# Lag rows of an S5 mixer fetched within on-chip memory, contraction rows by channel then row, later factor sums as plain DMA sums

## The chip, the cores and the metric

The kernel runs on one core of one Trainium2 chip. The metric is the device time of one execution in microseconds (us). A core has TensorE (PE; its weight loads are listed apart as PEld), VectorE (DVE), ScalarE (ACT), GpSimd (POOL) and SyncE (SP), which work through separate instruction queues and wait for each other by semaphores. DMAs are issued from the queues of SP, ACT and POOL.

## The reference, cut to what matters

One layer of a backbone: an S5 mixer (a diagonal complex state-space model, run in both directions over 256 context and 1024 latent positions, 64 groups of 16 channels with 64 states each) with GELU and a gate, then a SwiGLU feed-forward part. The mixer's core:

```python
lam_bar = jnp.exp(lam * jnp.exp(log_step)[:, None])
b_bar = ((lam_bar - 1.0) / lam)[..., None] * lax.complex(b_re, b_im)
def run(u, h0):
    bu = jnp.einsum('lgh,gnh->lgn', u, b_bar)
    bu = bu.at[0].add(lam_bar * h0)
    a = jnp.broadcast_to(lam_bar, bu.shape)
    _, h = lax.associative_scan(_linear_combine, (a, bu), axis=0)
    return jnp.einsum('lgn,ghn->lgh', h, c_mat).real, h[-1]
...
y = y_forward + y_backward + d_skip * h
g = gelu(y)
g = g * sigmoid(g @ w_glu + b_glu)
...
return (silu(h @ w1) * (h @ w3)) @ w2
```

All data are float32, and around both parts stand RMS norms and shifts, scales and gates made from c and c_ctx through ada_w.

## The kernel before, in words

The 1024 latent positions are 128 chunks of T = 8 rows. A chunk's 8 rows by 16 channels of one group are 128 numbers, which is the contraction axis of the matmuls around the scan. So the recurrence goes over chunks, with powers of lam_bar to the 8th as steps, and what happens inside a chunk is done by matrices.

Four stages follow each other. **To 30 us** parameters and inputs are loaded. **30 to 121** prepares: powers of lam_bar, the input matrices (BL, made by bl_make at line 407 as products of a factor BXY, repeated over the 8 rows, and a power table LB or its bank copies LBP, repeated over the 16 channels), their transposes, and the chunk inputs of the scan. Of the products of 128x1024, those of the hb values in PMUL run on POOL, the others on DVE. **121 to 221** is the scan: scan() (line 899) lays all its steps into DVE's queue, one dependent product and sum after another. Under it the other engines prepare what turns states into outputs. **221 to 252** takes the late half of the states, GELU and the transposes; **252 to 999** is the gate and the feed-forward part.

The order of the work under the scan is written out by hand in the string PROG1, of which each word is a step that issues its instructions on every engine concerned, and each engine takes its own in that order. PROG2 does the same behind the scan. The steps that matter here:

- C (cl_ops, line 679), on POOL: makes the output factors CL of quarter q, direction d. A group of five: a product, a product, an addition, a product, an addition. How the two additions are done is written in HOWS, two letters for each direction of each quarter: E is an operation on POOL, Y an accumulating DMA issued by POOL, P two pairs of matmuls with an identity on PE (line 693) that ACT copies back (line 694). q prepares the sum or difference of the factors of a quarter and, for q2, the power sums pw_sums(1) (line 620).
- K (k_mats, line 835), K0 to K7: two per quarter. PE computes from CL and BBn the impulse response of 16 channels for 15 lags, 240 numbers per row; ACT copies two such blocks from PSUM into the buffers KX (line 854) and stores them in a DRAM tensor kd (line 855).
- T (toeplitz, line 858), T0 to T15: SP loads from kd, over DRAM, the eight shifted windows of 128 numbers that make a 128 x 128 matrix of lags for four groups (line 863, 256 KB), into one of four KQ buffers in RA.
- P, P0 to P5: PE multiplies early states by CL (line 975, states_mm) and the chunk's own rows by KQ (line 999, x_mm); R copies states for it (line 955, ACT); Y copies the result out (line 1057, ACT). F fills in states on POOL. A computes adaLN rows on PE from ada_w pieces that SP loads (line 523). L loads the factors of C on ACT's queue (line 667).
- Behind the scan: Z copies the late half of the states (line 957 on DVE, 955 on ACT), N multiplies them by CL (line 975), D adds, H applies GELU (line 1066), I and J are transposes and Q covers groups 6 and 7.

SP's and ACT's DMAs share eight semaphores, which the program gives out in turn, in the order of the program text over both queues; a DMA waits until the one that had its semaphore before has landed.

Of the kernel before, what the change touches and what calls it, by code (L numbers as in the profile page):

```python
# [17 lines left out]
P = 128  # L18
# [24 lines left out]
def s5_ffn_kernel(tc, a, out):  # L43
# [3 lines left out]
    with ctx:  # L47
# [56 lines left out]
        modb = small([6, T])[:, 0:2]  # L104
        nrm = small([2, T])
        S5 = int(round(pos[0] * 256))
# [218 lines left out]
        S.activation(rsb, rsb, AF.Sqrt, bias=epsc[:, 0:1], scale=1.0 / D)  # L325
        LB = view(RC[2], 8, [2, T, P])

        def lb_dup(d, i, pt):

            pt = pt.rearrange("p (s g) -> p s g", s=T)  # L330
            PE.matmul(pt, cid[:, d], CP[:, :, i] if d else CP[:, ::-1, i], start=True, stop=True)
            S.activation(LB[:, i, :, G * d:G * d + G], pt, AF.Copy, scale=sgn[:, 0:1] if i else 1.0)

# [62 lines left out]

        BL1 = [view(RC[1], 4 * i, [8, T, HC]) for i in range(3)] + [view(RC[0], 8 + 4 * i, [8, T, HC]) for i in range(2)]
        BL2 = [view(r, kb, [8, T, HC]) for r, kb in ((RC[1], 12), (RXc, 4), (RC[3], 4))]
        Win = [view(RC[r], kb, [2, 4, P]) for r, kb in ((3, 0), (2, 0), (2, 4))]
        BB = view(RC[3], 8, [2, G, HC])  # L400

        def bls(hb):
            return BL1[hb % 5], BL2[hb % 3]

        def bl_make(hb, o2=None):

            if hb >= 16:
                return
            b, d = bd(hb)
            es = slice(64 * d + 8 * b, 64 * d + 8 * b + 8)  # L410
            for i in range(2):
                l_ = bc((LBP[hb][:, i] if hb in LBP else LB[:, i, :, es]).rearrange("p s g -> p g s"), 3, HC)
                tt(o2 if i and o2 is not None else bls(hb)[i], bc(BXY[:, b // 2 % 2, i, d, 8 * (b % 2):8 * (b % 2) + 8], 2, T), l_, MUL, E if hb in PMUL else V)

        LBP = {}

        def lb_psum(hb, eng=V):

            n, o = {0: (0, 0), 2: (0, 128), 4: (1, 384), 7: (0, 0), 9: (0, 128), 11: (1, 384), 12: (2, 384), 14: (0, 0),
                    15: (0, 128)}[hb]  # L420
            bank = (lbt, LTa, tq)[n]
            b, d = bd(hb)
            LBP[hb] = bank[:, o:o + 128].rearrange("p (i s g) -> p i s g", i=2, s=T)
            src = LB[:, :, :, 64 * d + 8 * b:64 * d + 8 * b + 8]
            if eng is S:
                S.copy(LBP[hb], src)
            else:
                eng.tensor_copy(LBP[hb], src)
# [8 lines left out]
        def bl_tr(hb, copy=True):  # L437
            b, d = bd(hb)
            t1 = bls(hb)[0]
            pt, w_ = pv2(), Win[hb % 3]  # L440
            for j in range(2):
                for i in range(4):
                    PE.transpose(pt[:, j, P * i:P * i + P], t1[:, 4 * j + i].rearrange("p s h -> p (s h)"), ident)
            if not copy:
                return pt, w_
            if hb == 15:
                S.copy(w_[:, 0].rearrange("p i n -> p (i n)"), pt[:, 0])
                V.tensor_copy(w_[:, 1].rearrange("p i n -> p (i n)"), pt[:, 1])
            else:
                S.copy(w_.rearrange("p j i n -> p (j i n)"), pt.rearrange("p j n -> p (j n)"))  # L450
            bb_copy(hb)

        def bb_copy(hb):
            b, d = bd(hb)
            S.copy(BB[:, d, 8 * b:8 * b + 8], bls(hb)[0][:, :, 7 if d == 0 else 0])

# [86 lines left out]
        pr0 = pv2()  # L543
        o2 = pr0.rearrange("p j (i s h) -> p (j i) s h", i=4, s=T)
        bl_make(0, o2)
# [127 lines left out]
        def cs_sum(q):  # L673
            c0, c1, c2 = (Cs[q % 2][:, i].rearrange("p d g h -> p (d g h)") for i in range(3))
            tt(c2, c0, c1, SUB, E)

        MB = view(RXa, 0, [D])

        def cl_ops(q, d):
# [8 lines left out]
            def add(o, how, last):  # L688
                if how == "P":
                    for h in range(2):  # L690
                        hs, pc = slice(4 * h, 4 * h + 4), pw([512])
                        for i, src in enumerate((o, ct)):
                            PE.matmul(pc, ident, src[:, hs].rearrange("p g t h -> p (g t h)"), start=i == 0, stop=i == 1)
                        S.activation(o[:, hs].rearrange("p g t h -> p (g t h)"), pc, AF.Copy, scale=-1.0 if last else 1.0)
                elif how == "Y":
                    E.dma_start(o, ct, accum_op=ADD)
                else:
                    tt(o, o, ct, SUB if last else ADD, E)

# [135 lines left out]
        def k_mats(q, hq, kts):  # L835
# [16 lines left out]
            for g_ in range(2):  # L852
                gq, kx = 2 * hq + g_, KX[2 * hq + g_]
                S.copy(kx, kts[g_])
                S.dma_start(KD_[q][:, gq], kx)

        def toeplitz(u):

            q, gi = divmod(u, 4)
            rows = KD_[q][32 * gi:32 * gi + HC]  # L860
            n = 15 * HC
            src = bass.AP(rows.tensor, rows.offset, [[HC, T], [n, 4 * HC], [1, P]])
            SY.dma_start(KQ[u % 4], src)

# [143 lines left out]
        def run(prog):  # L1008


            for w in prog.split():
# [784 lines left out]
def layouts(i):  # L1796
# [3 lines left out]
    ident = np.eye(P, dtype=np.float32)  # L1800
    blk = np.kron(np.eye(8, dtype=np.float32), np.ones((HC, HC), np.float32))
# [4 lines left out]
    sel = np.tile(np.eye(HC, dtype=np.float32), (8, 8))  # L1806
    msk = np.kron(np.eye(8, dtype=np.float32), np.ones((HC, 1), np.float32))
# [42 lines left out]
```

## Time and profile before

| | us |
|---|---|
| median of 3 runs | 1009.99 |
| lowest and highest | 1006.97, 1013.54 |
| the profiled execution | 1006.91 |
| its span, first to last instruction | 1005.1 |
| mean granted TensorE clock | 0.984 |
| busy: PE, PEld | 952.8, 751.5 |
| busy: DVE, POOL, ACT | 774.3, 748.7, 427.7 |

The profile is of one execution. A row of a group gives line, engine, operation, tiles written and read (buffer numbers left out), the shapes, the count, the busy time, the mean duration in ns and the idle time of the engine just before such instructions, with what ended it. L77 is the helper tt, through which almost all elementwise operations go, so groups of L77 are told apart by their tiles. A timeline row begins with its start and its length, and an idle time in brackets stands before it. ACTq, SPq and POOLq are issues of DMAs.

### The profile page before, as it was taken

Reading aid. Unit: us, or ns where it says so; the run is one execution under the profiler, and the core shown is the slowest. Engines: PE = TensorE matmul, PEld = TensorE weight load, DVE = VectorE, ACT = ScalarE, POOL = GpSimd, SP = SyncE. Lnnn points to the kernel's source line nnn. Section 1 sums busy time; section 2 is a strip of 40 time slices with the busy share of each in tenths; the row PEclk is TensorE's granted clock in tenths of the full one; section 3 lists DMA queues with packets and bytes.
Section 4 is the critical chain, followed back from the end, with each engine's and each line's share of the span. In section 5 each row is a group of like instructions: output and inputs, shape, how many; then the busy total and the mean of one; then the engine's idle time right before and its main releaser. Section 6 shows DMA issues by size and latency. Waiting matters only on the chain. (4 is left out here: it accounts for less than half of the span.)

```text
span 1005.1 us, 17726 instructions
## 1 busy us (share of the span) xinstructions
PE 952.8 (95%) x6604; PEld 751.5 (75%) x6604; DVE 774.3 (77%) x1630; ACT 427.7 (43%) x808; POOL 748.7 (74%) x595
## 2 busy tenths in 40 slices
PE   5987898879999999999999999999999999999996
PEld 1466535769888778778888888888888888888885
DVE  7979899984556778878869586685958677686977
ACT  5478622224434563343233343434243343334337
POOL 5799998963734458979786869777785878777764
PEclk9999998889999999999999999999999999999999
DMA  9765998535520032011212121111212120111205
GB/s 335 285 133 108 287 316 273 125 85 171 210 64 22 1 105 84 11 43 42 74 53 74 42 79 34 47 61 45 74 42 84 43 64 32 61 55 53 74 22 167
DMA packets 49118, 99.95 MB, mean 99 GB/s; under 512 B 4348, under 2 KB 18940, under 8 KB 47752
## 3 DMA queue, kind: packets, MB, share of 16 engines
q1 hardware_dynamic: 43416, 86.64, 26.1%
q0 software_dynamic: 2592, 9.44, 5.1%
q10 hardware_dynamic: 3024, 2.74, 0.9%
q8 instruction: 52, 0.85, 0.3%
q14 instruction: 34, 0.28, 0.1%
HBM read 83.20 MB, written 6.17 MB: 89 GB/s over the span
## 5 line engine op out<-in xcount | busy, mean ns | idle before, releaser
L77 POOL TENSOR_TENSOR c<-rxc,c 128x512 fp32r<-128x512 f32 x127 | 166.0, 1320 | 52.3 <-ACT c L1305 51.5
L1364 PE MATMUL ut<-ra,c 128*128 128x512 f32 x400 | 155.7, 389 | 1.2 <-DVE ra L77 1.2
L1363 PE MATMUL ut<-ra,c 128*128 128x512 f32 x400 | 155.7, 389 | 0.2 <-ACT ra L1305 0.2
L1365 PE MATMUL ut<-ra,c 128*128 128x512 f32 x400 | 155.6, 389 | 0.0
L1305 ACT CAST c<-rxc 128x512 fp32r<-128x512 f32 x128 | 79.0, 622 | 147.6 <-PE xt L1658 53.0
L1658 PE MATMUL xt<-c,c 128*128 128x512 f32 x540 | 129.7, 389 | 0.0
L77 DVE TENSOR_TENSOR ru<-ru,xt 128x1024 f32<-128x1024 f32 x90 | 107.9, 1216 | 13.4 <-PE xt L1658 9.4
L1658 PEld LDWEIGHTS xt<-c,c 128*128 128x128 f32 x540 | 101.4, 188 | 21.0
L77 DVE TENSOR_TENSOR ru<-ut,ru 128x512 f32<-128x512 f32 x98 | 67.2, 686 | 44.1 <-PE ut L1365 38.6
L1364 PEld LDWEIGHTS ut<-ra,c 128*128 128x128 f32 x400 | 75.1, 188 | 17.1 <-POOL rxc L77 1.5
L1363 PEld LDWEIGHTS ut<-ra,c 128*128 128x128 f32 x400 | 75.1, 188 | 16.1 <-ACT ra L1305 0.6
L1365 PEld LDWEIGHTS ut<-ra,c 128*128 128x128 f32 x400 | 75.1, 188 | 15.6
L77 POOL TENSOR_TENSOR c<-ru,c 128x512 fp32r<-128x512 f32 (+1 forms) x39 | 58.8, 1507 | 10.1 <-ACT c L1305 5.7
L77 POOL TENSOR_TENSOR rxc<-rxc 128x512 f32<-128x512 f32 (+1 forms) x44 | 63.8, 1450 | 2.2 <-ACT rxc L671 0.6
L77 POOL TENSOR_TENSOR c<-rw,c 128x512 fp32r<-128x512 f32 (+1 forms) x28 | 37.4, 1337 | 37.5 <-ACT c L1305 37.5
L1363 PE MATMUL ut<-c,c 128*128 128x512 f32 x160 | 62.3, 390 | 0.8 <-DVE rxa L77 0.8
L1364 PE MATMUL ut<-c,c 128*128 128x512 f32 x160 | 62.3, 389 | 0.0
L1365 PE MATMUL ut<-c,c 128*128 128x512 f32 x160 | 62.2, 389 | 0.0
L1658 PE MATMUL ut<-c,c 128*128 128x512 f32 x216 | 51.9, 389 | 0.0
L77 DVE TENSOR_TENSOR ru<-ru,ut 128x512 f32<-128x512 f32 x76 | 47.3, 680 | 0.7 <-ACT ru L1712 0.5
L1658 PEld LDWEIGHTS ut<-c,c 128*128 128x128 f32 x216 | 40.5, 188 | 8.4
L587 PE MATMUL pv<-ru,c 128*64 128x160 f32 x512 | 41.4, 312 | 5.2 <-ACT c L450 2.0
(453 smaller groups left out, 2392.0 us busy)
## 6 DMA issues: line engine op xcount, KB each, us to landing
c<-in_ada_w SPq DMA_DIRECT2D x46, 256.0 KB, 5.9
rxc<-in_w SPq DMA_DIRECT2D x38, 256.0 KB, 2.9
rxc<-in_w SPq DMA_DIRECT2D x19, 512.0 KB
c<-c POOLq DMA_DIRECT2D x11, 512.0 KB, 5.7
ru<-in_w SPq DMA_DIRECT2D x11, 512.0 KB
rw<-in_w SPq DMA_DIRECT2D x11, 512.0 KB, 3.6
ra<-in_ada_w SPq DMA_DIRECT2D x10, 512.0 KB, 10.8
ra<-in_ada_w SPq DMA_DIRECT2D x18, 256.0 KB, 8.8
```

Of the source, the lines that this page charges most:

```text
L77: eng.tensor_tensor(out=o, in0=x, in1=y, op=op)
L587: PE.matmul(pv[64 * (i % 2):64 * (i % 2) + 64, ri, c0:c0 + 160], w[:, i, 64 * ri:64 * ri + 64], U[:, 8 * b + 4 * j + i], start=True, stop= ...
L1305: S.copy(o[0], x)
L1363: PE.matmul(pu, wh, bh, start=start, stop=False)
L1364: PE.matmul(pu, wh, bl, start=False, stop=False)
L1365: PE.matmul(pu, wl, bh, start=False, stop=stop)
L1658: PE.matmul(pd, w[:, cs_], b, start=j in (1, 2, 4) and n == 0, stop=n == 2, skip_group_check=j not in (1, 2, 4))
```

## The change

The lag rows no longer pass through DRAM. KX becomes two buffers that hold both blocks of one K step (in R0 and RW), and 64 DMAs of 64 KB fetch the shifted windows from there straight into KQ; T and t words (groups hq 0 and 1) issue them on SP, and the new words e (behind K0) and f (behind K1) issue the first sixteen on ACT. The tensor kd is gone. For this the 128 contraction rows are ordered by channel, then row, where they were by row, then channel: in LB, BL1, BL2, LBP, bl_make's broadcasts, the views around transposes, and the tables xT, ctxT, blk and sel, which are laid out before the kernel starts. HOWS uses DMA additions in quarters 2 and 3 where it had operations on POOL or matmuls; there the factors are prepared with signs that make every addition plain. The power sums of quarters 2 and 3 (word n1) are issued earlier and take two operations on POOL and a negation on ACT where they took four on POOL. Words of PROG1 stand in another order.

```diff
-HOWS = "YPYP EPEP YEYE YPYE"
+HOWS = "YPYP EPEP YYYY YYYE"
...
-PROG1 = ("A22 G1 B0 A26 A30 C01 O0 C03 q1 A34 K0 O1 A38 A42 C10 C11 K1 O2 L2 A46 A50 C12 C13 A54 K2 O3 A58 T0 T1 T2 T3 F10 F11 G2 R0 K3 L3 R1 P0 Y0 Y1 A64 M0 P1 T4 T5 R2 Y2 Y3 G3 q2 C20 T6 T7 C21 P2 R3 Y4 Y5 C22 M1 P3 Y6 Y7 C23 q3 C30 K4 K5 R4 T8 T9 T10 T11 C31 C32 C33 F30 F31 P4 R5 Y8 Y9 K6 P5 Y10 Y11 K7 T12 T13 T14 T15 w0 l1 M2 m0 w1")
+PROG1 = ("A22 G1 B0 A26 A30 C01 O0 C03 q1 A34 K0 e0 e1 e2 e3 O1 A38 A42 C10 C11 K1 O2 L2 f0 f1 f2 f3 A46 A50 C12 C13 n1 A54 K2 O3 A58 F10 F11 G2 R0 K3 L3 R1 P0 Y0 Y1 T4 T5 t4 t5 A64 M0 P1 R2 Y2 Y3 T6 T7 t6 t7 G3 q2 C20 C22 C21 P2 R3 Y4 Y5 M1 P3 Y6 Y7 C23 q3 C30 K4 T8 T9 T10 T11 K5 t8 t9 t10 t11 R4 C31 C32 C33 F30 F31 P4 R5 Y8 Y9 K6 T12 T13 P5 Y10 Y11 T14 T15 K7 t12 t13 t14 t15 w0 l1 M2 m0 w1")
...
-        LB = view(RC[2], 8, [2, T, P])
+        LB = view(RC[2], 8, [2, P, T])
...
-        BL1 = [view(RC[1], 4 * i, [8, T, HC]) for i in range(3)] + [view(RC[0], 8 + 4 * i, [8, T, HC]) for i in range(2)]
+        BL1 = [view(RC[1], 4 * i, [8, HC, T]) for i in range(3)] + [view(RC[0], 8 + 4 * i, [8, HC, T]) for i in range(2)]
...
-                l_ = bc((LBP[hb][:, i] if hb in LBP else LB[:, i, :, es]).rearrange("p s g -> p g s"), 3, HC)
-                tt(o2 if i and o2 is not None else bls(hb)[i], bc(BXY[:, b // 2 % 2, i, d, 8 * (b % 2):8 * (b % 2) + 8], 2, T), l_, MUL, E if hb in PMUL else V)
+                l_ = bc(LBP[hb][:, i] if hb in LBP else LB[:, i, es], 2, HC)
+                tt(o2 if i and o2 is not None else bls(hb)[i], bc(BXY[:, b // 2 % 2, i, d, 8 * (b % 2):8 * (b % 2) + 8], 3, T), l_, MUL, E if hb in PMUL else V)
...
-            tt(PS[i], PWF[:, :, 0, :, gs], PWF[:, :, 1, :, gs], ADD, E)
-            if i == 0:
-                tt(PWF[:, :, 1, :, gs], PWF[:, :, 1, :, gs], PWF[:, :, 0, :, gs], SUB, E)
-            else:
-                for d, gs, neg in ((slice(0, 2), slice(16, 24), True), (slice(0, 1), slice(24, 32), False), (slice(1, 2), slice(24, 32), True)):
-                    re, im = PWF[:, :, 0, d, gs], PWF[:, :, 1, d, gs]
-                    tt(im, re if neg else im, im if neg else re, SUB, E)
+            re, im = PWF[:, :, 0, :, gs], PWF[:, :, 1, :, gs]
+            tt(PS[i], im, re, SUB if i else ADD, E)
+            tt(im, im, re, ADD if i else SUB, E)
+            if i:
+                S.activation(im, im, AF.Copy, scale=-1.0)
...
-            tt(c2, c0, c1, SUB, E)
+            tt(c2, c0, c1, ADD if q > 1 else SUB, E)
...
-        KX = [cpk[:, HC + P:HC + P + 15 * HC], cols.rearrange("p a b g -> p (a b g)")[:, 0:15 * HC]]
-        KX += [view(RW, 4 + i, [15 * HC]) for i in range(2)]
+        KX = [R0[:, 32 + P:32 + P + 30 * HC], view(RW, 4, [30 * HC])]
+        KX = [t.rearrange("p (g x) -> p g x", g=2) for t in KX]
         KQ = [view(RA, STB * (2 + i // 2) + 2 * (i % 2), [4, P]) for i in range(4)]
-        KD_ = [dr.tile([P, 4, 15 * HC], F32, tag=f"kd{q}", name=f"kd{q}") for q in range(4)]
...
-                gq, kx = 2 * hq + g_, KX[2 * hq + g_]
-                S.copy(kx, kts[g_])
-                S.dma_start(KD_[q][:, gq], kx)
-
-        def toeplitz(u):
-
-            q, gi = divmod(u, 4)
-            rows = KD_[q][32 * gi:32 * gi + HC]
-            n = 15 * HC
-            src = bass.AP(rows.tensor, rows.offset, [[HC, T], [n, 4 * HC], [1, P]])
-            SY.dma_start(KQ[u % 4], src)
+                S.copy(KX[hq][:, g_], kts[g_])
+
+        def toeplitz(u, hq, eng=SY):
+
+            for g_ in range(2):
+                rows = KX[hq][32 * (u % 4):32 * (u % 4) + HC, g_]
+                src = bass.AP(rows.tensor, rows.offset, [list(rows.ap[0]), [HC, T], [1, P]])
+                eng.dma_start(KQ[u % 4][:, 2 * hq + g_], src)
...
-                    toeplitz(i)
+                    toeplitz(i, int(op in "tf"), S if op in "ef" else SY)
```

Three places of the queues show how the rows move. In the rows below c_63 to c_66 are the four 16 KB regions that hold the factors, r_60 is a parameter region, kt and pw are PSUM tiles; line numbers of the changed kernel are smaller by 2 to 8 from line 620 on.

On ACT, behind the matmuls of K0. Before:

```order
L854 COPY r_60<-kt 128x240
L855 DMA kd_1250<-r_60 128x240
L854 COPY r_60<-pw 128x240
L855 DMA kd_1250<-r_60 128x240
L804 COPY pw<-r_60 128x240
L694 ACTIVATE c_64<-pw 128x512 x2
```

Now:

```order
L850 COPY r_60<-kt 128x240
L850 COPY r_60<-pw 128x240
L857 DMA ra<-r_60 128x1x128 x8
L802 COPY pw<-r_60 128x240
L692 ACTIVATE c_64<-pw 128x512 x2
```

Two stores give way to eight fetches, which stand ahead of the zeroing of the next PSUM tile (802) and the copies of the next P addition (692).

On POOL, the two directions of quarter 2. Before:

```order
L77 TENSOR_TENSOR c_66<-rxc,rxa 128x1024
L77 TENSOR_TENSOR c_65<-rxc 128x1024
L696 DMA c_65<-c_66 128x1024
L77 TENSOR_TENSOR c_65<-rxc,rxa 128x1024
L77 TENSOR_TENSOR c_65<-c_65,c_66 128x1024
L77 TENSOR_TENSOR c_66<-rxc,rxa 128x1024
L77 TENSOR_TENSOR c_65<-rxc 128x1024
L696 DMA c_65<-c_66 128x1024
L77 TENSOR_TENSOR c_65<-rxc,rxa 128x1024
L77 TENSOR_TENSOR c_65<-c_65,c_66 128x1024
```

Now:

```order
L77 TENSOR_TENSOR c_66<-rxc,rxa 128x1024
L77 TENSOR_TENSOR c_65<-rxc 128x1024
L694 DMA c_65<-c_66 128x1024
L77 TENSOR_TENSOR c_66<-rxc,rxa 128x1024
L77 TENSOR_TENSOR c_65<-rxc 128x1024
L694 DMA c_65<-c_66 128x1024
L77 TENSOR_TENSOR c_65<-rxc,rxa 128x1024
L694 DMA c_65<-c_66 128x1024
L77 TENSOR_TENSOR c_65<-rxc,rxa 128x1024
L694 DMA c_65<-c_66 128x1024
```

The two additions on POOL are DMAs, and the first halves of both directions come ahead of the second halves. In quarter 3 one more DMA takes the place of the matmuls below.

On PE, between K5 (its last two matmuls are the first two rows; pm and kt are its PSUM tiles) and K6. Before:

```order
L850 MATMUL kt<-rxc,rxa 16x16
L850 MATMUL pm<-rxc,rxa 16x16
L693 MATMUL pw<-c_66,r_60 128x512
L693 MATMUL pw<-ra,r_60 128x512
L693 MATMUL pw<-c_66,r_60 128x512
L693 MATMUL pw<-ra,r_60 128x512
L975 MATMUL pw<-c_65,ra 64x128 x32
L999 MATMUL pw<-ra,ru 128x128 x8
```

Now:

```order
L847 MATMUL kt<-rxc,rxa 16x16
L847 MATMUL pm<-rxc,rxa 16x16
L967 MATMUL pw<-c_65,ra 64x128 x32
L991 MATMUL pw<-ra,ru 128x128 x8
L839 MATMUL kt<-c_66,rxa 16x112
L839 MATMUL pm<-c_66,rxa 16x112
```

P4 (967, 991) follows K5 at once, and K6 (839) follows P4 as before. DVE's rows are the same in the same order in both kernels.

More of the change, by code (lines that the diff above doesn't have):

```diff
@@ L96, in small @@
             return v
+        nrm = small([2, T])
         cpk = small([HC + 3 * P + HC + 4 + T + 16 + 8])
@@ L104, in s5_ffn_kernel @@
         modb = small([6, T])[:, 0:2]
-        nrm = small([2, T])
         S5 = int(round(pos[0] * 256))
@@ L331, in lb_dup @@
             PE.matmul(pt, cid[:, d], CP[:, :, i] if d else CP[:, ::-1, i], start=True, stop=True)
-            S.activation(LB[:, i, :, G * d:G * d + G], pt, AF.Copy, scale=sgn[:, 0:1] if i else 1.0)
+            S.activation(LB[:, i, G * d:G * d + G].rearrange("p g s -> p s g"), pt, AF.Copy, scale=sgn[:, 0:1] if i else 1.0)
         for i in range(2):
@@ L395, in bd @@
             return divmod((0, 2, 1, 3)[hb] if hb < 4 else hb, 2)
-        BL1 = [view(RC[1], 4 * i, [8, T, HC]) for i in range(3)] + [view(RC[0], 8 + 4 * i, [8, T, HC]) for i in range(2)]
-        BL2 = [view(r, kb, [8, T, HC]) for r, kb in ((RC[1], 12), (RXc, 4), (RC[3], 4))]
+        BL1 = [view(RC[1], 4 * i, [8, HC, T]) for i in range(3)] + [view(RC[0], 8 + 4 * i, [8, HC, T]) for i in range(2)]
+        BL2 = [view(r, kb, [8, HC, T]) for r, kb in ((RC[1], 12), (RXc, 4), (RC[3], 4))]
         Win = [view(RC[r], kb, [2, 4, P]) for r, kb in ((3, 0), (2, 0), (2, 4))]
@@ L422, in lb_psum @@
             b, d = bd(hb)
-            LBP[hb] = bank[:, o:o + 128].rearrange("p (i s g) -> p i s g", i=2, s=T)
-            src = LB[:, :, :, 64 * d + 8 * b:64 * d + 8 * b + 8]
+            LBP[hb] = bank[:, o:o + 128].rearrange("p (i g s) -> p i g s", i=2, s=T)
+            src = LB[:, :, 64 * d + 8 * b:64 * d + 8 * b + 8]
             if eng is S:
@@ L442, in bl_tr @@
                 for i in range(4):
-                    PE.transpose(pt[:, j, P * i:P * i + P], t1[:, 4 * j + i].rearrange("p s h -> p (s h)"), ident)
+                    PE.transpose(pt[:, j, P * i:P * i + P], t1[:, 4 * j + i].rearrange("p h s -> p (h s)"), ident)
             if not copy:
@@ L454, in bb_copy @@
             b, d = bd(hb)
-            S.copy(BB[:, d, 8 * b:8 * b + 8], bls(hb)[0][:, :, 7 if d == 0 else 0])
+            S.copy(BB[:, d, 8 * b:8 * b + 8], bls(hb)[0][:, :, :, 7 if d == 0 else 0])
         r4, mx = view(RA, 74, [4, P]), view(RA, 76, [2, 2, 32])
@@ L543, in s5_ffn_kernel @@
         pr0 = pv2()
-        o2 = pr0.rearrange("p j (i s h) -> p (j i) s h", i=4, s=T)
+        o2 = pr0.rearrange("p j (i h s) -> p (j i) h s", i=4, s=T)
         bl_make(0, o2)
@@ L693, in add @@
                             PE.matmul(pc, ident, src[:, hs].rearrange("p g t h -> p (g t h)"), start=i == 0, stop=i == 1)
-                        S.activation(o[:, hs].rearrange("p g t h -> p (g t h)"), pc, AF.Copy, scale=-1.0 if last else 1.0)
+                        S.activation(o[:, hs].rearrange("p g t h -> p (g t h)"), pc, AF.Copy, scale=-1.0 if last and q < 2 else 1.0)
                 elif how == "Y":
@@ L697, in add @@
                 else:
-                    tt(o, o, ct, SUB if last else ADD, E)
+                    tt(o, o, ct, ADD, E)
             h0, h1 = HOWS.split()[q][2 * d:2 * d + 2]
@@ L1026, in run @@
                     cs_sum(i)
-                    if i == 2:
-                        pw_sums(1)
+                elif op == "n":
+                    pw_sums(i)
                 elif op == "B":
@@ L1040, in run @@
                     fill(*divmod(i, 10), *((RXc, 0) if i >= 30 else (RC[3], 12)))
-                elif op == "T":
-                    toeplitz(i)
+                elif op in "Ttef":
+                    toeplitz(i, int(op in "tf"), S if op in "ef" else SY)
                 elif op == "R":
@@ L1800, in layouts @@
     ident = np.eye(P, dtype=np.float32)
-    blk = np.kron(np.eye(8, dtype=np.float32), np.ones((HC, HC), np.float32))
+    blk = np.kron(np.ones((HC, HC), np.float32), np.eye(8, dtype=np.float32))
     pat = np.tile(np.eye(HC, dtype=np.float32), (8, 1))
@@ L1805, in layouts @@
     sg[:64, 1], sg[64:, 1] = 1, -1
-    sel = np.tile(np.eye(HC, dtype=np.float32), (8, 8))
+    sel = np.tile(np.repeat(np.eye(HC, dtype=np.float32), 8, 1), (8, 1))
     msk = np.kron(np.eye(8, dtype=np.float32), np.ones((HC, 1), np.float32))
@@ L1823, in layouts @@
     a["x"] = c(f["x"][0])
-    a["xT"] = c(f["x"].reshape(P, T, G, HC).transpose(1, 3, 2, 0).reshape(P, G, P))
-    a["ctxT"] = c(f["ctx"].reshape(32, T, G, HC).transpose(1, 3, 2, 0).reshape(P, G, 32))
+    a["xT"] = c(f["x"].reshape(P, T, G, HC).transpose(3, 1, 2, 0).reshape(P, G, P))
+    a["ctxT"] = c(f["ctx"].reshape(32, T, G, HC).transpose(3, 1, 2, 0).reshape(P, G, 32))
     a["ada_w"] = c(f["ada_w"][0])
```

## The prediction, on record before the run

> **What bounds the kernel now.** I read the windows of the four stages first, then the groups of VectorE in the stage that the edits touch, then the chain of waits of TensorE and the timeline of three engines around that stage's end. In the windows the columns are: from and to, length, then the busy time of PE, PEld, DVE, ACT and POOL, the granted TensorE clock, the share of the DMA engines and GB/s.
>
> ```profile
> 30.00:121.00 91.00, 75.72 (x744) 53.57 (x744) 81.54 (x192) 63.88 (x142) 85.19 (x95) 0.98 0.71 183
> 121.00:221.00 100.00, 88.51 (x1708) 53.20 (x1701) 99.45 (x559) 25.75 (x56) 92.28 (x80) 0.88 0.73 217
> 221.00:252.00 31.00, 29.27 (x833) 28.12 (x810) 13.10 (x23) 14.54 (x21) 9.19 (x9) 1.00 0.50 147
> 252.00:999.00 747.00, 740.67 (x3310) 611.23 (x3308) 554.03 (x742) 307.18 (x570) 547.94 (x398) 1.00 0.19 61
> ```
>
> TensorE is busy for 740.67 of the last 747 us, and no instruction of that stretch is edited. Nearly all that the change edits lies under 121 to 221, where VectorE, the scan, is busy for 99.45 of 100 us. Its two largest shapes show that it waits for nobody (the last column is the idle time ahead of them):
>
> ```profile
> L77 DVE TENSOR_TENSOR ltc<-ra,lta 128x128 f32<-128x128 f32 x92 | 26.7, 290 | 0.0
> L77 DVE TENSOR_TENSOR ltb<-ra,lta 128x128 f32<-128x128 f32 x92 | 26.6, 289 | 0.1
> ```
>
> So 100 us of this stage are VectorE's alone, and what TensorE, ScalarE, GpSimd or a DMA saves under it can show only at its end. There:
>
> ```profile
> 220.82 0.29 DVE L77 TENSOR_TENSOR ra<-ltc,ra 128x128 f32<-128x128 f32 x1
> 221.25 0.76 DVE L957 COPY ra<-ra 128x512 f32<-128x512 f32 x2
> ```
> ```profile
> 222.39 0.36 ACT L854 COPY rw<-kt 128x240 f32<-128x240 f32 x1 [0.78 <-PE pm L850]
> ...
> 223.59 0.47 ACTq L855 DMA_DIRECT2D kd<-rw  x1
> 224.11 1.14 ACT L955 COPY ra<-ra 128x512 f32<-128x512 f32 x2 [0.54 <-ACT rw L854]
> ```
> ```profile
> 222.81 1.32 PE L975 MATMUL pe<-c,ra 64*64 64x128 f32 x33 [0.47 <-ACT rw L854]
> 224.97 7.26 PE L975 MATMUL pe<-c,ra 64*64 64x128 f32 x227 [0.85 <-issue]
> ```
>
> The scan ends at 221.1. The last work under it, K7, is copied out at 222.39, and the first late product N0 begins at 222.81 after a wait for that copying. N0 needs Z0, the first of the two copies on DVE: 221.25 plus half of 0.76 is 221.63. TensorE is thus about 1.1 us behind the scan at the handover, and this little, not the 100 us, is open to the change.
>
> **The change part by part.** *Lag rows.* Sixteen stores into kd and sixteen loads from it go. TensorE waited for them as follows:
>
> ```profile
> PE pw L999 <- DMA ra<-kd: 5.5, 4, 3.6
> ```
> ```profile
> 209.43 2.08 PE L999 MATMUL pw<-ra,ru 128*128 128x128 f32 x8 [3.55 <-DMA ra<-kd]
> 212.12 2.08 PE L999 MATMUL pw<-ra,ru 128*128 128x128 f32 x8 [0.61 <-DMA ra<-kd]
> ```
>
> 5.5 us in all, 3.55 and 0.61 of it in P4, the only place after which the end of K7 can move. In their place come 64 copies of 64 KB within SBUF. No such copy stands in the trace; the nearest rows are these (durations of an issue as least, median, most):
>
> ```profile
> L863 SPq DMA_DIRECT2D ra<-kd x16: 574/640/3513, 166.5 to 228.3; - x16
> L855 ACTq DMA_DIRECT2D kd<-rw x8: 326/326/940, 153.2 to 223.6; - x8
> ```
> ```profile
> DMA to landing us min/median/max: 2.7/3.3/5.0
> ```
> ```profile
> c<-in_ada_w SPq DMA_DIRECT2D x46, 256.0 KB, 5.9
> ra<-in_ada_w SPq DMA_DIRECT2D x18, 256.0 KB, 8.8
> ```
>
> An issue costs between 0.33 and 0.64 us, a landing between 2.7 us (the least of the 120 KB stores) and 8.8 us. I take 0.4 and 4, near the store, since that also leaves SBUF in short rows and is the closer in size. One hop in place of store and load then ends P4's two waits.
>
> The Trainium skill, "DMA: Bandwidth & Descriptors", section "Rules for kernel authors", speaks against this edit: many small transfers should be put together, and under 64 KB one pays mostly overhead. Its section "Bandwidth" gives 0.95 us for 64 KB; eight in a row would by that estimate land 7.6 us after the first began, which would give P4 its wait back but still leave K7 about where it was, and the sum no gain. No trace here shows such a copy.
>
> *The sums.* TensorE loses the four matmuls of the one addition that stands between K5 and P4, at half clock:
>
> ```profile
> 197.74 2.08 PE L693 MATMUL pw<-c,r 128*128 128x512 f32 x2 [0.57 <-POOL c L77]
> ...
> 203.62 0.41 PE L975 MATMUL pw<-c,ra 64*64 64x128 f32 x4
> ```
>
> That is 5.9 us. GpSimd, busy 92.28 of 100, loses two additions and gains three DMA issues:
>
> ```profile
> L77 POOL TENSOR_TENSOR c<-c,rw 128x1024 f32<-128x1024 f32 x2 | 4.7, 2356 | 0.2
> L696 POOL DMA_DIRECT2D c<-c x3 | 2.6, 875 | 0.9 <-POOL c L77 0.6 <-DMA ra<-kd 0.3
> L77 POOL TENSOR_TENSOR rxa<-rxa 128x64 f32<-128x64 f32 x2 | 0.6, 320 | 0.0
> L77 POOL TENSOR_TENSOR rxa<-rxa 128x128 f32<-128x128 f32 x1 | 0.5, 454 | 0.1
> ```
>
> 2 x 2.36 less 3 x 0.88 is 2.1 us saved, and the power sums, four operations now two and a negation on ScalarE, save some 0.4 more. Nobody on the path waits for that; the cover is the scan. The new wait is that K4 to K7 now read sums that a DMA finishes, and that landing takes:
>
> ```profile
> c<-c POOLq DMA_DIRECT2D x4, 512.0 KB, 7.8
> ...
> c<-ra POOLq DMA_DIRECT2D x1, 512.0 KB, 4.7
> ```
>
> K4 stands behind P2 and P3 in TensorE's order; before K6 the very last step stays an addition on GpSimd. I let 0 to 3 us of it reach TensorE.
>
> *ScalarE's queue.* Eight fetches each now sit in it after K0 and K1, ahead of the evacuations that TensorE needs for C11, K1 and C13. The program hands all hardware DMAs eight semaphores in turn over both queues, so each of the 16 waits until the DMA eight before it has landed, and those ahead are the 256 KB loads above. Sixteen issues of 0.33 to 0.64 are 5.3 to 10.2 us against 16 issues of kd stores saved later (5.2); waits for landings come on top. I put TensorE 0 to 8 us late at K2 to P3, 4 taken.
>
> *K7's end* is then 222.3 - 5.9 - 3.55 - 0.6 = 212.2, plus 0 to 8 for ScalarE's queue and 0 to 3 for the landings: 212 to 223, taken 216 to 217. In most of this span TensorE ends before the scan, and the waits that were removed come back as one idle stretch in front of N0.
>
> *The order of rows.* Same sizes on every engine; the two broadcast operands of the products of 128x1024 change places, so that now the first one repeats along the innermost axis. There are 18 of them on DVE in the second stage (10 of the next row's kind, and eight with other tiles):
>
> ```profile
> L77 DVE TENSOR_TENSOR c<-c,lbt 128x1024 f32<-128x1024 f32 x10 | 11.9, 1218 | 4.1 <-DMA c<-c 3.3 <-DVE lbt L428 0.4
> L77 DVE TENSOR_TENSOR ra<-ltb,r 128x64 f32<-128x64 f32 x4 | 0.7, 219 | 0.1
> L77 DVE TENSOR_TENSOR ra<-ra,ltb 128x64 f32<-128x64 f32 x4 | 0.9, 214 | 0.0
> ```
>
> The second row (the scales spread at line 473) already repeats its first operand along the innermost axis and takes 219 ns against 214 of a plain one of its size. Ends: nothing, or at worst 18 x 1.22 = 22 us if each took double. I take nothing, by the near row.
>
> *After the scan.* Gains: N0 at 221.7 and not 222.81, 1.1 us. ScalarE's second pair of state copies, held to 224.11 behind K7's copies and stores, can follow the scan at once, so that the idle 0.85 inside N0 should go too: 1.95 together, as the upper end 2.4 with a further issue gap of 0.41 at 240.3.
>
> ```profile
> PE pe L988 <- issue: 0.4, 1, 0.4
> ```
>
> Against it stands the clock:
>
> ```profile
> 168.20:171.60 3.40, 3.40 (x64) 3.12 (x64) 3.40 (x21) 1.30 (x3) 3.40 (x3) 0.50 0.69 198
> 205.70:209.10 3.40, 0.18 (x6) 0.00 (x0) 3.26 (x16) 0.00 (x0) 3.40 (x4) 1.00 0.63 134
> 209.10:212.50 3.40, 2.46 (x10) 2.16 (x11) 3.40 (x21) 0.00 (x0) 3.24 (x6) 0.51 0.58 148
> 212.50:215.90 3.40, 3.40 (x97) 3.14 (x98) 3.40 (x21) 1.08 (x2) 3.32 (x6) 0.50 0.20 58
> 215.90:219.30 3.40, 3.40 (x132) 3.25 (x132) 3.40 (x21) 0.72 (x2) 3.22 (x7) 0.99 0.14 40
> 222.80:226.20 3.40, 2.54 (x72) 2.46 (x76) 0.00 (x0) 2.44 (x4) 0.00 (x0) 1.00 0.23 75
> ```
> ```profile
> 216.47 2.27 PE L975 MATMUL pw<-c,ra 64*64 64x128 f32 x64
> ```
>
> A stretch of 3.4 us with almost no matmul (205.7) is followed by two at half clock, while one with 2.54 of 3.4 is not. 64 matmuls of one kind take 3.40 us at 0.50 and 2.27 at 0.99, so a third of the time at half clock is lost. If TensorE idles from 216.5 to 221.7, the start of N0 runs at half clock for one to two stretches, 3.4 to 6.8 us, and 1.1 to 2.3 us are lost, 1.7 in the middle. The Trainium skill, "TensorE: Matmul & The Clock Gate", Part 1, has the windows free-running; which of the two ends comes is then left to their phase, which this trace doesn't settle for another kernel.
>
> **Sum.** -1.1 - 0.85 + 1.7 = -0.25 us, with ends at -2.4 (no half clock, all gaps gone) and +1.2 (2.3 lost, only 1.1 gained). The profiled execution took 1006.91 us (span 1005.1 and 1.8 around it): 1006.7. It is 3.1 below the median of the runs, 1009.99, and I see no part of that difference that the change would take away; so 1009.7 for a median.
>
> **Rivals.**
> A. *No half clock*: K7 ends only after 218 or so, or the idle stretch does not fill a window. Then -2.0 to -2.4, 1007.7. For it: landings of 7.8 us above, which would hold K6. Against: 10 us have been taken from TensorE's chain.
> B. *ScalarE's queue sets the end* (slower): the sixteen waiting fetches push K1 to K7 later than the scan by themselves. This decides once the delays exceed the 10 us removed less the 1.2 us lag, about 9; with landings of 8.8 us met twice, 17.6 us late, K7 would end at 229.8 and N0 start seven us late, less the 0.85: +6, 1016. For it: ScalarE has evacuations of TensorE behind these waits. Against: the scan's slack absorbs the first nine.
> C. *The broadcast in the other operand is slow*: 22 us on DVE before the scan, +22, 1032. Against: the row of 219 ns.
> D. *The kernel before loses time in some runs to the trip over DRAM* (its runs spread over 6.6 us), and the change removes that: 1007. Nothing in one profile can show it.
>
> **How the numbers follow.** A measurement of this kernel tells about 1% from no change, 10.1 us. The main case has 0.60, A 0.12, D 0.14, B 0.09, C 0.04, and 0.01 is left for a gain before the scan that I don't see. Main, A and D lie within 1%; of B a quarter goes beyond, C wholly. So faster 0.01, same 0.93, slower 0.06. The range goes from 1004.5 (the lowest run, 1006.97, less 2.4) to 1015 (the highest run, 1013.54, plus 1.2, and just short of B).
>
> **What would show it.** Right: no TensorE wait for a DMA in P4; K7's last copy near 217 and an idle stretch of 4 to 9 us that ends at Z0; half clock after it; the scan ending at 221 as before; the last stage unchanged. Wrong: K7's copies after 221 again (A, or B with a ScalarE that waits for DMAs between 147 and 170), the 128x1024 products above 1.22 us (C), or a scan that ends more than 1 us earlier or later, since nothing of the sum allows that.

## The result, and the profile after

The changed kernel is slower: 1014.62 us median of 19 runs (1009.08 to 1022.08) against 1007.03 for the kernel before (1004.14 to 1013.54, 19 runs), a ratio of the means of 1.0065 with a 95% interval of 1.0047 to 1.0084, or 4.7 to 8.5 us. The time lies inside the range given, by 0.4 us, but the forecast of no change doesn't hold: the loss is small and clear. The profiled execution took 1015.43, with a span of 1013.7 against 1005.1.

The windows of the changed kernel, with the columns as above, for the scan and for the stretch behind it:

```profile
121.00:221.00 100.00, 78.91 (x1426) 44.64 (x1418) 99.39 (x557) 21.71 (x50) 84.76 (x69) 0.85 0.80 208
221.00:252.00 31.00, 28.66 (x863) 26.96 (x866) 12.77 (x21) 15.02 (x22) 8.12 (x14) 1.00 0.54 134
```

VectorE is as busy under the scan as before. TensorE got 78.91 us of work done there and not 88.51. A part of that is the matmuls of the addition that is gone; but from 221.00 to N0 at 232.75 TensorE is still busy for 9.71 us with the rest of P4, with K6, P5 and K7, which stood under the scan before but for the end of K7. The ends of the three engines' work there:

```profile
220.10 0.29 DVE L77 TENSOR_TENSOR ra<-ltc,ra 128x128 f32<-128x128 f32 x1
220.52 1.75 DVE L949 COPY ra<-ra 128x512 f32<-128x512 f32 x2
```
```profile
222.36 1.29 ACT L1049 COPY ru<-pw 128x512 f32<-128x512 f32 x2 [6.60 <-PE pw L991]
...
232.34 0.36 ACT L850 COPY rw<-kt 128x240 f32<-128x240 f32 x1 [0.97 <-ACT ru L1049]
232.59 0.36 ACT L850 COPY rw<-pm 128x240 f32<-128x240 f32 x1
```
```profile
232.75 1.56 PE L967 MATMUL pe<-c,ra 64*64 64x128 f32 x41 [0.52 <-ACT rw L850]
```

The scan ends at 220.4, a little earlier than before. K7's last copy starts at 232.6 where it started at 223.2, and N0, which waits for the first of K7's two copies, starts at 232.75 (222.81 before). So the whole loss is this: TensorE's work under the scan no longer fits under it. The chain of waits names two kinds of waiting that are new or larger; the columns are engine and line, releaser, us in total, times, longest:

```profile
PE pw L991 <- DMA ra<-rw: 9.5, 6, 3.3
...
ACT c L692 <- DMA ra<-rw: 9.8, 1, 9.8
...
ACT pw L802 <- DMA ra<-r: 7.6, 1, 7.6
```

TensorE waits 9.5 us for lag rows (5.5 before), though they now make one hop and not two. ScalarE stands for 7.6 and 9.8 us at the two places where it issues fetches. Of TensorE's 9.5 us, 8.8 lie in P2 and P3, whose copies out on ScalarE stand apart as they never did before:

```profile
189.27 0.58 ACT L1049 COPY ru<-pw 128x512 f32<-128x512 f32 x1 [3.22 <-PE pw L991]
193.26 0.58 ACT L1049 COPY ru<-pw 128x512 f32<-128x512 f32 x1 [3.41 <-PE pw L991]
...
202.87 0.58 ACT L1049 COPY ru<-pw 128x512 f32<-128x512 f32 x1 [8.50 <-PE pw L991]
206.11 0.59 ACT L1049 COPY ru<-pw 128x512 f32<-128x512 f32 x1 [2.65 <-PE pw L991]
```

The first and second of a pair are four and three us apart; in the kernel before both copies of a step follow each other. The issues of the fetches and their landings (least, median, most):

```profile
L857 SPq DMA_DIRECT2D ra<-r x24: 544/550/2096, 176.8 to 230.9; - x24
L857 SPq DMA_DIRECT2D ra<-rw x24: 544/592/1808, 180.5 to 238.3; - x24
```
```profile
DMA to landing us min/median/max: 2.3/3.3/8.6
```

Most of the fetches are quick, some are four times slower. How the DMA engines are shared says when. These are the queues from 181 to 193 us, where P2 and P3 need their rows (those of P0 and P1 come with the first sixteen fetches), before and after; q0 is GpSimd's accumulating DMAs, q1 SyncE's queue:

```profile
q1 hardware_dynamic: 1741, 0.88, 24.5%
q0 software_dynamic: 144, 0.52, 22.8%
```
```profile
q0 software_dynamic: 415, 1.53, 67.6%
q1 hardware_dynamic: 996, 0.46, 28.8%
```

The additions moved 0.52 MB there before and 1.53 MB now, on two thirds of the engines' time, while what SyncE's queue moved in that stretch fell from 0.88 to 0.46 MB.

The gaps that these waits leave are followed by half clock. From 198.4 to 205.2 TensorE is busy for 0.83 and 0.59 us of two stretches of 3.4, and in the four stretches that follow, to 218.8, the granted clock is 0.50: K4, K5 and the first part of P4 run there. The kernel before has half clock under the scan too, around other gaps, so the mean from 121 to 221 falls only from 0.88 to 0.85.

### The profile page after: what moved, and what is told of

The parts are those of the page before. It is cut to its first block, busy times and chain, and to the rows that moved or that the text cites. A ratio compares the mean times of both kernels' runs of the same rounds, so it can differ in the third digit from the quotient of the medians.

```text
span 1013.7 us, 17785 instructions
## 1 busy us (share of the span) xinstructions
PE 951.1 (94%) x6596; PEld 749.8 (74%) x6596; DVE 779.6 (77%) x1630; ACT 429.3 (42%) x807; POOL 744.2 (73%) x594
## 5 line engine op out<-in xcount | busy, mean ns | idle before, releaser
L77 DVE TENSOR_TENSOR ru<-ru,xt 128x1024 f32<-128x1024 f32 x90 | 107.1, 1214 | 10.1 <-PE xt L1650 7.5
L1355 PEld LDWEIGHTS ut<-ra,c 128*128 128x128 f32 x400 | 75.1, 188 | 16.2 <-ACT ra L1297 0.6
L77 POOL TENSOR_TENSOR c<-ru,c 128x512 fp32r<-128x512 f32 (+1 forms) x39 | 56.6, 1452 | 10.1 <-ACT c L1297 5.7
```

What stands on the lines that cost most here:

```text
L77: eng.tensor_tensor(out=o, in0=x, in1=y, op=op)
L1355: PE.matmul(pu, wh, bh, start=start, stop=False)
```

## The experiments

Two theories were set against each other. **Q**: ScalarE's queue, blocked by the sixteen fetches, makes all that follows late. **C**: the added accumulating DMAs crowd the fetches out on the DMA engines that all queues share. **F**, a weaker form of C, puts the price on the fetches themselves, their number or their issue. The table gives, for the profiled execution of each kernel, when the last listed copy out of a step starts on ScalarE (us), and the ratio of the times with its interval.

| kernel | P0 | P1 | P3 | K5 | P4 | K7 | ratio |
|---|---|---|---|---|---|---|---|
| before | 174.3 | 181.4 | 191.2 | 198.1 | 213.8 | 223.2 | 1 |
| changed | 178.1 | 184.1 | 206.1 | 214.4 | 222.4 | 232.6 | 1.0065 [1.0047, 1.0084] |
| e1 fetches on SyncE | 181.9 | 187.9 | 208.1 | 216.2 | 223.0 | 234.9 | 1.0100 [1.0072, 1.0127] |
| e2 old sums | 175.4 | 181.4 | 193.5 | 201.6 | 211.7 | 221.4 | 0.9979 [0.9962, 0.9997] |
| e3 before, new sums | 174.7 | 181.5 | 191.4 | 208.3 | 221.7 | 232.3 | 1.0072 [1.0045, 1.0099] |
| e5 half the fetches | 173.5 | 179.5 | 189.4 | 197.1 | 204.3 | 213.7 | 0.9964 [0.9945, 0.9983] |
| e6 half the bytes | 176.9 | 182.9 | 197.1 | 207.4 | 213.9 | 223.4 | 0.9988 [0.9971, 1.0005] |
| e7 new sums in quarter 3 | 178.5 | 184.5 | 195.9 | 204.1 | 215.1 | 225.5 | 1.0007 [0.9992, 1.0021] |
| e8 new sums in quarter 2 | 179.5 | 185.5 | 205.6 | 212.6 | 219.8 | 229.9 | 1.0042 [1.0025, 1.0060] |
| e9 before, new sums, early n1 | 178.0 | 185.9 | 204.5 | 213.7 | 225.0 | 235.4 | 1.0069 [1.0042, 1.0095] |
| e10 first sixteen later | 188.0 | 193.6 | 203.4 | 209.7 | 219.3 | 229.4 | 1.0053 [1.0036, 1.0071] |
| e11 first sixteen left out | 173.0 | 179.0 | 198.9 | 207.9 | 214.5 | 224.4 | 1.0004 [0.9988, 1.0019] |
| e12 half of each addition | 175.6 | 181.6 | 193.1 | 202.2 | 211.4 | 221.4 | 0.9988 [0.9972, 1.0003] |
| e13 quarter 2 on GpSimd | 180.0 | 186.0 | 195.9 | 202.3 | 214.5 | 226.3 | 0.9995 [0.9980, 1.0010] |

Executions differ by up to four us already at K0, ahead of all that is edited here (the start of its last copy lies between 145.1 and 149.1), so differences within a row say more than those between rows.

**e1, the queue.**

```diff
-                    toeplitz(i, int(op in "tf"), S if op in "ef" else SY)
+                    toeplitz(i, int(op in "tf"), SY)
```

> The first sixteen fetches are issued by SyncE instead of ScalarE, at the same places of the program. Theory Q (ScalarE's queue, blocked for 7.6 and 9.8 us behind K0 and K1, makes all that follows late): ScalarE's copies of K1 come near 153 us, P0 ends 4 us earlier, K7's last copy moves from 232.6 to about 222 to 225, and the time falls by 6 to 8 us, to that of the kernel before within 2 us. Theory F (the fetches themselves are the bound: 0.55 us of issue at the least, 1.2 to 2.1 us and landings of 4 to 8 us while other DMAs run): K0 to P0 gain their 4 us, P2 and P3 wait for their fetches until the same times as now (P3's copies out at 203 and 206), K7 ends at 231 to 234 and the time stays within 2 us of the changed kernel.

It became no faster, and rather slower (the two intervals overlap), as theory Q did not have it. K1 is copied out at 154.2, as theory Q has it, but P0 comes 3.8 us later than in the changed kernel. SyncE's queue also holds the ada_w loads, and now they stand behind fetches that wait for K0 and K1; TensorE's weight loads wait for them, 14.1 us and not 6.1:

```profile
PEld pm L534 <- DMA c<-in_ada_w: 14.1, 12, 3.0
```

So the run can't clear or convict ScalarE's block, which it only moved to another queue. e11 says more.

**e2, the old sums** (the fetches as changed).

```diff
-HOWS = "YPYP EPEP YYYY YYYE"
+HOWS = "YPYP EPEP YEYE YPYE"
```

> The table of additions of the kernel before (YEYE and YPYE), the rest as changed: three accumulating DMAs fewer in quarters 2 and 3, two additions on GpSimd and one on TensorE more. Theory C (the accumulating DMAs crowd the fetches of P2 and P3 out, and are the larger loss): landings of the fetches of P2 and P3, now 3.8 to 8.7 us, fall below 4.5, P3's last copy out comes before 201 (206 now), K7's end gains 3 us or more in spite of the 3 to 6 us for the matmuls' addition between K5 and P4, where TensorE waits for its fetches anyway. Theory F: P3 stays within 2 us of 206, K7's end and the time within 2 us of the changed kernel.

P3 comes at 193.5 and not 206.1, one wait of TensorE for lag rows is left, and the time falls to 1005.86 against 1008.46 for the kernel before, run beside it: faster by 0.3 to 3.8 us, a small gain. This is the version that beats both.

```profile
PE pw L991 <- DMA ra<-rw: 2.0, 1, 2.0
```

Its K7 and N0, in which the scan's end and TensorE's work meet:

```profile
221.43 0.36 ACT L850 COPY rw<-pm 128x240 f32<-128x240 f32 x1
```
```profile
221.59 1.31 PE L967 MATMUL pe<-c,ra 64*64 64x128 f32 x33 [0.52 <-ACT rw L850]
223.41 9.22 PE L967 MATMUL pe<-c,ra 64*64 64x128 f32 x287 [0.51 <-issue]
```

N0 starts 1.2 us earlier than before and the gap inside it is 0.51 and not 0.85: the change without its sums gives most of what the prediction had put on the gain side (1.1 and 0.85), without the idle stretch.

**e5 and e6, the number or the bytes of the fetches.** Of e5, every second fetch left out:

```diff
-            for g_ in range(2):
+            for g_ in range(1):
```

> Every second fetch is left out (32 of 64 KB; groups of odd g_ keep old numbers in their buffers, so the output is another one). Theory F with the price on each DMA: the bursts on SyncE between 176 and 198 shrink from 21 to about 10 us, P3's last copy out comes 8 us or more earlier, K7 ends before 224, and the time comes to that of the kernel before or below it. Theory Q: ScalarE's blocks halve too, so K0 to P0 gain 2 to 4 us, which alone would end K7 near 229.

Of e6, 64 fetches of half as many bytes:

```diff
-                src = bass.AP(rows.tensor, rows.offset, [list(rows.ap[0]), [HC, T], [1, P]])
-                eng.dma_start(KQ[u % 4][:, 2 * hq + g_], src)
+                src = bass.AP(rows.tensor, rows.offset, [list(rows.ap[0]), [HC, T], [1, 64]])
+                eng.dma_start(KQ[u % 4][:, 2 * hq + g_, 0:64], src)
```

> All 64 fetches, each of 128 rows of 256 bytes and not 512 (the second half of each lag row keeps old numbers, so the output is another one). If the price is on each DMA (issue, and its turn at one of the eight semaphores): nothing moves, K7 ends at 231 to 234. If it is on the bytes: as in the run with every second fetch left out, K7 ends before 226.

With the same 64 issues, half the bytes bring P3 from 206.1 to 197.1 and K7 from 232.6 to 223.4. That is against F with a price on each DMA. Half the count does more (P3 at 189.4, K7 at 213.7). A part of that is ScalarE's block, which it shortens too: P0 comes 3.4 us earlier than in e6, P3 7.7. e5 is the only run in which TensorE is clearly done ahead of the scan, and it shows the idle stretch that the prediction feared. The windows of e5 around the scan's end, and its N0:

```profile
215.90:219.30 3.40, 0.00 (x0) 0.00 (x0) 3.40 (x21) 0.00 (x0) 0.00 (x0) 0.65 0.84 203
219.30:222.70 3.40, 1.70 (x28) 1.56 (x32) 2.28 (x10) 1.80 (x3) 0.00 (x0) 0.50 0.98 355
222.70:226.10 3.40, 3.40 (x72) 3.40 (x68) 0.84 (x2) 0.63 (x1) 0.00 (x0) 0.50 0.76 272
```
```profile
221.00 12.95 PE L967 MATMUL pe<-c,ra 64*64 64x128 f32 x320 [7.66 <-DVE ra L77]
```

Two stretches at half clock, and 320 matmuls in 12.95 us that take 10.5 in e2 (1.31 and 9.22): 2.4 us lost, just above the 1.1 to 2.3 that were forecast for such a case. K7 nine us earlier than in the kernel before was worth only 1.7 to 5.5 us of time.

**e3 and e9, the new sums without the new fetches**: the kernel before with the sums of the change. In e3 the power sums stay at their old place behind q2; e9 moves them as the change does.

```diff
-HOWS = "YPYP EPEP YEYE YPYE"
+HOWS = "YPYP EPEP YYYY YYYE"
```

With it go the signs and the power sums as in the diff of the change; e9 adds the word n1 behind C13.

> The kernel before with the sums of the change alone (its signs, the power sums and seven accumulating DMAs in quarters 2 and 3 in place of four); lag rows still go over DRAM, in the old order. Theory C (a DMA that moves lag rows lands behind an accumulating DMA that runs at the same time, so each added accumulation under P2 to P4 delays TensorE, whatever way the rows take): the loads from kd get later too, TensorE's wait for kd grows from 5.5 us to 9 or more, K7's last copy comes 3 us or more after 223.2, and the time is 1010 to 1016. If the sums are harmless by themselves and only the 64 small fetches suffer from them: K7 ends before 223, because the matmuls' addition is gone, and the time is 1005 to 1009.

e3 was slower by 0.72%, but not for the reason given: its wait for kd was 5.9 us, hardly more than 5.5, and P3 came as before. GpSimd stood behind the negation that the new power sums put into ScalarE's queue:

```profile
183.29 2.02 POOL L77 TENSOR_TENSOR c<-rxc,rxa 128x1024 f32<-128x1024 f32 x1 [9.62 <-ACT rxa L627]
```

That made K4 late. TensorE then waited in K4 for the landing of the late sums:

```profile
PE kt L840 <- DMA c<-c: 7.2, 2, 3.8
```

This is the wait that the prediction had priced at 0 to 3 us; here it shows, while none stands among TensorE's waits in the changed kernel. GpSimd's wait behind the negation is a price which the change avoids by moving n1. So theory C was tried again without it:

> As the kernel before with the sums of the change, but the power sums and their negation on ScalarE are issued behind C13, where the change has them; in the first such run GpSimd stood 9.6 us behind that negation, which hid the question. Theory C (lag rows and accumulating DMAs share the DMA engines, whatever way the rows take): TensorE's wait for kd grows above 5.5 us, and K4 and P4 come late, K7's last copy after 225 and the time above 1009. If only the 64 small fetches suffer: kd's wait stays within 1 us of 5.5, K7 ends at 215 to 222, since the matmuls' addition is gone, and the time is 1004 to 1008.

```profile
PE pw L997 <- DMA ra<-kd: 12.4, 8, 3.2
```

The loads over DRAM suffer as the fetches do: TensorE waits 12.4 us for kd, and the time is as long as that of the whole change. The sums alone thus cost as much, whatever way the rows take. Not each us of it is the added DMAs': P0 comes 3.7 us later, before the first of them runs, and 3.25 us of the wait for kd stand there; GpSimd stood 7.1 us behind TensorE ahead of the second addition; and the profiled execution, 1017.58, was 3.6 us above the median. From P1 to P3 it takes 18.6 us and not 9.9, and that part fits the additions.

**e7 and e8, one quarter each.**

```diff
-HOWS = "YPYP EPEP YYYY YYYE"
+HOWS = "YPYP EPEP YEYE YYYE"
```

> The changed kernel with the old additions in quarter 2 (YEYE) and the new ones in quarter 3 (YYYE). Theory C, with the loss in quarter 2, whose accumulations stand at 175 to 195, just where P2 and P3 fetch: P3's last copy out comes at 194 as with the old sums, K4 to P4 lose a few us to the three accumulations of quarter 3 (193 to 208) but TensorE has no addition there; K7 ends between 214 and 222, the time is 1003 to 1007. If the addition in quarter 3 were the harmful one: P3 at 194, but K7 after 226 and the time above 1009.

For e8 the table reads "YPYP EPEP YYYY YPYE".

> The other half: new additions in quarter 2 (YYYY), old ones in quarter 3 (YPYE). Theory C with the loss in quarter 2: P3's last copy out at 203 to 207 as in the changed kernel, fetches of P3 that land 4 to 8 us after their issue, K7 near 232 or later (the matmuls' addition is back), the time 1012 to 1018. Otherwise: P3 before 198 and the time below 1009.

With new sums in quarter 2 alone P3 is at 205.6, as in the whole change; with those of quarter 3 alone at 195.9. e8's time, 1011.23, and its K7 were a little better than expected. e7's time, 1007.94, was above what was expected, no better than the kernel before: its K7 comes at 225.5 where 214 to 222 were expected. The three additions of quarter 3 run just while P4's rows are fetched, and of the 4.7 us of waiting for rows that remain, 3.4 stand in P4. In both runs the waits for rows stand beside or just behind the added DMAs of their quarter.

**e10 and e11, ScalarE's block.** In e10 (old sums) the words e0 to f3 were replaced by T0 to T3 and t0 to t3 behind A58.

> The changed kernel with the old additions, and the first sixteen fetches on SyncE behind the last ada_w loads but one, where the kernel before has its loads from kd. ScalarE is blocked no more (7.7 and 8.3 us with the old additions and fetches on ScalarE). If that block cost time: K1 is copied out at 153 and not at 155.5, P0 comes 1 to 3 us earlier than 175.4 or, with sixteen issues of 0.6 us behind one another from 166 on, up to 3 us later; K7 ends before 221 or just at it, and the time stays within 2 us of that with the old additions alone, because the scan on VectorE then ends last in either.

This run can't answer its question, and K7 (229.4) and the time came out later than expected. K2 writes its rows over those of K0 before T0 to T3 read them, so a half of the rows that P0 and P1 take are other ones; and K3, which writes over those of K1, had to wait 18.5 us for the fetches t0 to t3. Nothing follows from it on ScalarE.

In e11 the eight words are dropped, all else as changed.

> The changed kernel without the first sixteen fetches (P0 and P1 read old numbers, so the output is another one); the other 48, and all new sums, stay. Theory Q (ScalarE's block sets the end): K1 near 153, P0 4 us earlier than 178.1, P3 before 200, K7 before 224, the time back at that of the kernel before. Theory C: K1 to P1 gain their 4 us or more, but the fetches of P2 and P3 still land behind the accumulations of quarter 2, P3's last copy out stays after 202, K7 after 228, and the time within 3 us of the changed kernel.

P0 comes 5.1 us earlier than in the changed kernel, and P1 to P3 still take 19.9 us (22.0 in the change, 9.8 before), with 6.5 us of waiting for rows. P3 (198.9), K7 (224.4) and the time, back at that of the kernel before, are near what theory Q had and not theory C, though P1 to P3 stay slow. So the first sixteen fetches, ScalarE's block and the transfers together, cost about 5 us at P0, and the end feels them because the additions have used up the scan's slack; in e2 the block is there too (7.7 and 8.3 us), and the kernel is still no slower than before. The two causes add up, and leaving out either one is enough.

**e12 and e13, the additions' own work.** In e12 the seven DMAs of quarters 2 and 3 remain, each with half of its bytes:

```diff
-                    E.dma_start(o, ct, accum_op=ADD)
+                    E.dma_start(*((o[:, 0:4], ct[:, 0:4]) if q > 1 else (o, ct)), accum_op=ADD)
```

> The changed kernel in which each of the seven accumulating DMAs of quarters 2 and 3 adds only the first half of its rows (256 KB and not 512; the other half is left unsummed, so the output is another one). Same issues on GpSimd, same 64 fetches. Theory C (the accumulating DMAs' own work on the shared DMA engines holds up the fetches): their landings fall from 5 to 8 us to 3 to 5, the fetches of P3 land 2.5 to 5 us after issue, P3's last copy out comes from 206 to 195 to 200, K7 from 232.6 to 221 to 227, the time is 1004 to 1009. If the number of DMAs or the sums' order were the cause: P3 stays after 203 and the time above 1011.

Half of the accumulated bytes, with the same issues, order and fetches, gives nearly the times of e2: P3 at 193.1, K7 at 221.4, 1.8 us of TensorE's waits for rows left of 9.5; its N0 in the timeline:

```profile
221.58 1.53 PE L967 MATMUL pe<-c,ra 64*64 64x128 f32 x40 [0.52 <-ACT rw L850]
```

This is the plainest proof of C for P2 and P3: it is the bytes of the additions that hold the rows up. From 176 to 207 us GpSimd's queue used 63.2% of the DMA engines' time in the changed kernel, 36.4% in e2, and 35.2% in e12 with about as many packets as in the changed kernel (in this order; packets, MB, share):

```profile
q0 software_dynamic: 991, 3.67, 63.2%
```
```profile
q0 software_dynamic: 573, 2.09, 36.4%
```
```profile
q0 software_dynamic: 1008, 1.84, 35.2%
```

e13's table is "YPYP EPEP EEEE YPYE":

> The changed kernel with no accumulating DMA at all in quarter 2 (EEEE) and the old additions in quarter 3 (YPYE). Theory C: the fetches of P1 too, which with the old additions still landed 3.0 to 7.4 us after issue, land in 2.3 to 3 us; P1 comes 1 us or more earlier than 181.4 or stays if it waits for nothing there, P3 stays near 193.5. GpSimd pays 2 x 2.36 less 2 x 0.62, 3.5 us more in quarter 2, so K4 is 0 to 3.5 us later than 196.9; the time is that of the old additions within 2 us, 1004 to 1008.

The eight fetches issued behind P0 serve P2; those of P1 are among the first sixteen, so the expectation names the wrong step. They land in 2.4 to 2.9 us (median 2.6), against 2.7 to 4.5 (3.7) in e12, 3.5 to 7.4 (5.8) in e2 and 3.7 to 8.6 (6.2) in the changed kernel. P1 to P3 take 9.9 us, as in the kernel before. K0 was 3.8 us later than in e2 in this execution; that and the two more operations on GpSimd may account for K7's 226.3 and for a time no better than before, which is not shown.

## Why the prediction was wrong, step by step

*What bounds the kernel*: right. The scan ended within 1 us of where it was, the last stage is unchanged, and all of the loss lies in the handover, N0 9.9 us later (of which the span shows 8.6). That little was to be gained was right too: e2, which has the fetches without the sums, gains 0.3 to 3.8 us.

*ScalarE's queue*, 0 to 8 us late, 4 taken: right. P0 came 3.8 us later in the changed kernel, and 5.1 us earlier again without the sixteen fetches.

*P4's two waits end and the matmuls' addition goes*, 10.1 us: nearly. Of 4.2 us of waits in P4, 0.6 are left; from K5 to P4 it took 15.7 us and takes 8.0, so 7.7 were saved, though K5 and a part of P4 now run at half clock. A fetch alone lands in 2.3 us, faster than the 4 taken, but eight in a row take 0.55 us of issue each and not 0.4.

*The sums*: this is the step that failed. The prediction asked who waits for the result of an added DMA, and let 0 to 3 us of it reach TensorE. It did not ask what else the DMA engines had to move in that time, though the rows that it quoted show 0.73 of them in use under the scan. From P1 to P3 it took 9.8 us and takes 22.0: 12 us in the place of at most 3. With half of the added bytes it takes 11.4 (e12) and with the old sums 12.1 (e2), so some 10 of the 12 us are the added bytes'; the other 2 go when quarter 2 has no accumulating DMA at all (9.9 in e13). So K7's last copy came at 232.6 and not near 217. From the first two rows of the table: 3.8 at P0, -1.1 from there to P1, 12.2 to P3, 1.4 to K5, -7.7 to P4 and 0.8 to K7 make the 9.4 us by which K7 is late.

*The clock and the order of rows*: N0 did not run at half clock, since TensorE was at work right up to it; the half clock came earlier, behind the waits of P2 and P3. e5 shows that its price was nearly right for a case in which TensorE idles ahead of N0. The products with the broadcast in the other operand take 1.22 us as before, so rival C is out:

```profile
L77 DVE TENSOR_TENSOR c<-c,lbt 128x1024 f32<-128x1024 f32 x10 | 11.9, 1219 | 3.8 <-DMA c<-c 3.0 <-ACT ra L597 0.2 <-PE pv L587 0.2
```

*Rival A* had the late K7 and the full clock in N0, but took the landings of the sums as the cause and saw a gain in it; K7 came far behind the scan, and it was a loss.

*Rival B* had the right sign and nearly the right time (1016), but named ScalarE's queue as the one that sets it. The block alone fits into the slack; it needs the additions beside it.

*Rival D*, that the trip over DRAM costs time in some runs only: e2's runs spread over 6.6 us as well, so nothing speaks for it.

That the time lies inside the range is luck. The range was built on three runs of the kernel before with a median of 1009.99, and 19 runs gave 1007.03; its upper end, 1015, is the highest of those three runs plus 1.2, and no term of it stands for held-up fetches.

The warning of the Trainium skill, "DMA: Bandwidth & Descriptors", section "Rules for kernel authors", against transfers under 64 KB, at whose edge these stand, did not decide here: with the old sums the kernel with 64 of them is a little faster than the one with 16 loads and 16 stores (e2, which differs from it in other points too). The 0.95 us for 64 KB that the prediction took from the Trainium skill, same page, section "Bandwidth", are measured there on loads from HBM into SBUF, issued by GpSimd; here the quickest landing took 2.3 us. Another line of the Trainium skill, in its section "Rules for kernel authors", does bear on it: transfers from two issuing engines share the same sixteen DMA engines, their packets interleaved. The trace agrees, in the 67.6% of GpSimd's queue beside 28.8% of SyncE's, together nearly all of the engines' time.

Left open: how much of the 22 us from P1 to P3 is landing and how much the longer issues on SyncE (up to 2.1 us), since both shrink together. The longer issues are a good part of it: from the first fetch of P2 to the end of the last issue for P3, SyncE's queue needed 22.7 us in the changed kernel, 16.9 in e2, 16.2 in e12 and 13.1 in e13.

## What to carry to other kernels

An addition moved from an engine to an accumulating DMA is not free because the engine is relieved: it takes time of the DMA engines, and the price is paid by whoever waits for another DMA in the same stretch. So list, for every DMA that is added, which transfers run beside it and who waits for them, as one lists the instructions behind a wait. And when work hides under a longer chain, sum all delays against the slack, not one by one: here 5 us of blocked queue and 12 us of held-up transfers stood against 8 us saved. Without the first (e11) or the second (e2) the kernel is no slower than before, with both it loses 6.5.

## What was not expected of the hardware

A 64 KB copy within SBUF took 0.55 us to issue and landed in 2.3 us at the least, and in 3.7 to 8.6 us beside the accumulating DMAs of 512 KB in the changed kernel (the eight behind P0); these themselves landed in 4.7 us (before) to 9.0 us (e9; medians of the groups of their kind). Issues of the copies grew in the same stretches from 0.55 to as much as 2.1 us. Halving the accumulated bytes brought the slowest landing of a fetch from 8.6 to 5.9 us (e12).
